# Gated DeltaNet in a hybrid recurrent step: the state chain gets a lane of its own, the block inverse moves into the preparation lane

## Chip, cores and metric

One NeuronCore of a Trainium2 chip runs the whole program. The metric is device time in microseconds (us), the median of several runs; lower is better. A profile of one execution, the trace, is read beside it.

## What is computed

One inference step of a two-layer trunk: 2048 prompt positions and 8 single-token samples, 1024 channels, float32. Layer 0 holds an RG-LRU and a gated DeltaNet as parallel groups of 8 heads behind one input projection and ahead of one output projection; layer 1 is an S5 state space layer. The change touches the DeltaNet of the prompt alone. For each head, with a decay `gc` (a running sum of log gates) and a factor `beta`:

```python
decay = exp(where(tri, gc[:, None] - gc[None, :], -inf))
A = where(strict, (k * beta) @ k.T * decay, 0)
u, w = solve(A + I, [v * beta, k * beta * exp(gc)])      # unit lower triangular
qk = where(tri, q @ k.T * decay, 0)
# chunk by chunk, S is the 128 x 128 state
v_new = u - w @ S
o = (q * exp(gc)) @ S + qk @ v_new
S = S * exp(g_last) + (k * exp(g_last - gc)).T @ v_new
```

## The kernel before

**Halves and heads.** The prompt is taken in two halves of 1024 positions. In layer 0 a half runs over 8 heads. Each head takes six units of the input projection in the order `k, xa, q, v, za, zb`, with the two gates of the RG-LRU (`lru`) between `za` and `zb`. A unit (`in_unit`) is 8 x 3 products of 128 x 128 weights with 1024 columns (1032 in the first half, with the 8 samples), since every float32 product is made of three products of high and low parts (`whi`, `wlo`; `hh`, `hl`). They are the matmuls at L840 into the PSUM tiles `ps_mm`. After the heads, `out_phase` runs 2 x 8 units of the output projection.

**Lanes.** Everything else is background: Python generators in the class `Fibers`, each in a lane. After every `BURST` = 1536 columns of a unit, `pump` advances the first generator of every lane by one `yield`; this is called a step here, and `wait(n)` is n steps. So a head of 6 x 24 x 1024 columns holds 96 steps. `drain` advances lanes to their end with no unit between the steps. Each engine takes its instructions in one fixed order, which a list scheduler makes of this program order.

**DeltaNet of a head** is in two generators. `gdn_prep` (lane `gp`) waits for `k`, transposes it (`ktok`), makes the decays `D`, the products `AT` (k with k) and `QKT` (k with q), each times `D`, then inverts the 16 x 16 diagonal blocks by forward substitution on VectorE (15 steps; `fsT`, `fsU`), writes them to scratch in HBM (`fst`), and reads them back in another layout by 16 small DMAs (`zt`, `zo`, `U32`), all on SyncE's queue. `gdn_main` (lane `gdn`) merges the inverse from blocks of 16 to 32, 64 and 128 by small matmuls into a tile `U`, and then goes over the 8 chunks, which depend on each other through the state `Sst`. At the end of each head stands `bg.drain("gp", "gdn")`; then `gdn_main` of this head is added, so that it runs during the next head.

**A chunk** is three hand-overs from TensorE to VectorE or ScalarE and back: p1 (L1094, L1095: k and q times the state), then `rr` on VectorE (L1097) and `qs` on ScalarE (L1100); two steps later p2 (L1103: the inverse times `rr`), then `wk` on VectorE (L1105) and `ww` on ScalarE (L1106); two steps later p3 (L1109, L1110), then the new state (L1111) and the output (L1112) on VectorE; three steps later the next chunk.

**Decays.** `decay_args` makes the exponents of the next head's `D` on VectorE (L874) behind the unit `za`, and the exponential is ScalarE's (L1157), in the middle of `lru`'s gate functions. The causal mask is put on `QKT` on GpSimd (`affine_select`, L949), behind VectorE's product at L948.

Of the kernel before, what the change touches and what calls it, by code (L numbers as in the profile page):

```python
# [26 lines left out]
DEC = 1  # L27
EVG = 3
# [5 lines left out]
class Fibers:  # L34
    """Background work, advanced step by step between bursts of the tensor engine."""
# [24 lines left out]
    def until(self, lane, flag, done):  # L60
        while flag not in done:
            self.step((lane,), True)
# [7 lines left out]
def hybrid_step(ctx: ExitStack, tc: tile.TileContext, I, O, dump=None):  # L70
# [46 lines left out]
    def in_order(*engines):  # L117
        """Each of these engines takes what the block traces in the order of the trace."""
# [19 lines left out]
    # ---------------------------------------------------------------- constants  # L138
# [25 lines left out]
    # ------------------------------------------------------------ small helpers  # L164
# [60 lines left out]
    # ------------------------------------------------------------- weight stream  # L225
# [50 lines left out]
    # --------------------------------------------------------------- parameters  # L276
# [115 lines left out]
    def make_h(i, xsrc, rows, hh, hl, permute, w):  # L392
        """h = rmsnorm(x) * w * (1 + scale) + shift, as two float32r parts."""
# [11 lines left out]
    def sample_norm(xs, name):  # L405
        """rstd of the sample rows, on every partition: [128, 8]"""
# [23 lines left out]
    # ---------------------------------------------------------------- S5 tables  # L430
    # Matrices of the 16-channel groups over 8 positions, kept in scratch by blocks of 8 groups.
# [22 lines left out]
    def s5_global():  # L454
# [35 lines left out]
        # powers 0..8 of the step  # L490
# [11 lines left out]
        # unit phases u^(2^j): j = 3 is the step of a chunk of 8  # L502
# [14 lines left out]
        # (A_bar - 1) / A  # L517
# [21 lines left out]
        # powers arranged by the rows' signs, in blocks of 8 groups  # L539
# [51 lines left out]
    def s5_tables(mt):  # L591
# [29 lines left out]
        for q in range(2):  # L621
# [28 lines left out]
            # phases of the chunks; the sine carries the rows' signs  # L650
# [30 lines left out]
    # ================================================================= layer 0  # L681
# [9 lines left out]
    tok = {n: K(n, (128, 8, 8)) for n in ("beta", "gc", "eg", "neg_eg", "egl", "ekap")}  # L691
# [19 lines left out]
    class Squares:  # L711
        """Sums of squares along the channels, by token columns."""
# [49 lines left out]
    def token_scalars(hf, Hh, Hl, blocks, wba):  # L762
# [41 lines left out]
        V.tensor_scalar(tok["neg_eg"], tok["eg"], -1.0, None, op0=OP.mult)  # L804
# [8 lines left out]
    def conv(dst, raw, wt, tile_i, silu, done=None):  # L813
        """the taps behind the last one"""
# [14 lines left out]
    def in_unit(hh, hl, blocks, evac, wts=None):  # L829
        """One block of 128 output channels; evac(first column, last column, sums)."""  # L830
# [18 lines left out]
    def raw_unit(unit, t, si, dst, wt, ti, bias=0.0):  # L849
        """channels before their convolution, and its last tap"""  # L850
# [14 lines left out]
    # ------------------------------------------------------------ gated DeltaNet  # L865
# [6 lines left out]
    def decay_args(dc, h):  # L872
        for c in range(8):
            V.tensor_scalar(dc[:, c], dc[:, c], tok["gc"][:, c, h:h + 1], 0.0, op0=OP.subtract, op1=OP.min)  # L874

    def gdn_prep(hf, h, g, ready):
        """Scalars, decayed products and inverses of the diagonal blocks of 16."""
# [29 lines left out]
        kap = g["kap"] = TT("gkap", S8)  # L907
# [1125 lines left out]
```

## Time and profile before

| | us |
|---|---|
| median of 3 runs | 3252.73 |
| lowest, highest | 3241.02, 3255.94 |
| span of the profiled execution, first to last instruction | 3234.9 |

The profile gives no time of its execution beside the span; the median is 17.8 us above it. Engines: PE is TensorE, PEld its weight loads, DVE VectorE, ACT ScalarE, POOL GpSimd, SP SyncE. In a view, "out<-in" names what an instruction writes and reads; an idle time in front of an instruction is put down to whoever released it last. "PEclk" is the clock granted to TensorE, as a share of 2.4 GHz.

### The profile page before, as it was taken

The numbers are of one execution on the slowest core, as the hardware profiler recorded it, in microseconds if no ns is written. First come the engines' busy times: TensorE is split into PE (matmuls) and PEld (weight loads), VectorE is DVE, ScalarE is ACT, GpSimd is POOL, SyncE is SP. The second block draws the span as 40 slices with busy tenths as digits, with TensorE's granted clock in tenths as the row PEclk, the third lists the DMA queues.
The fourth block names the chain that finished last, engine by engine and source line by source line (L and its number), as shares of the span: only waits on it lengthen the run. The fifth ranks groups of instructions, "written<-read, shape, count | busy, mean of one in ns | idle before, by whom it ended". The sixth has DMA issues, their size and how long they took to land. (4 is left out here: it accounts for less than half of the span.)

```text
span 3234.9 us, 53493 instructions
## 1 busy us (share of the span) xinstructions
PE 2980.9 (92%) x19958; PEld 2605.6 (81%) x19958; DVE 2207.5 (68%) x5420; ACT 1226.7 (38%) x2199; POOL 986.1 (30%) x872
## 2 busy tenths in 40 slices
PE   5898989999999999899999998999899999899998
PEld 3898988888888776677777777898888898778786
DVE  7887887578866777966776687445566734676634
ACT  3545544444443344534434444423111233211332
POOL 3224333333433424323323233322122223123231
PEclk8899999999999998999999999999999999999999
DMA  5132322322255532323322212433464414486322
GB/s 190 48 88 87 107 56 86 107 81 69 87 180 178 171 100 86 98 71 122 123 65 93 97 56 79 161 125 127 126 196 150 140 66 157 155 274 199 105 85 82
DMA packets 287780, 377.87 MB, mean 117 GB/s; under 512 B 97312, under 2 KB 165920, under 8 KB 287520
## 3 DMA queue, kind: packets, MB, share of 16 engines
q1 hardware_dynamic: 287520, 374.45, 35.6%
q8 instruction: 158, 2.59, 0.3%
q14 instruction: 102, 0.84, 0.1%
HBM read 276.73 MB, written 97.60 MB: 116 GB/s over the span
## 5 line engine op out<-in xcount | busy, mean ns | idle before, releaser
L218 POOL TENSOR_TENSOR wlo<-wraw,whi 128x512 fp32r<-128x512 f32 (+1 forms) x400 | 570.2, 1434 | 1207.3 <-ACT whi L217 729.9
L840 PE MATMUL ps_mm<-hh,wlo 128*128 128x512 f32 (+2 forms) x2536 | 793.2, 375 | 0.0
L840 PE MATMUL ps_mm<-hh,whi 128*128 128x512 f32 (+2 forms) x2536 | 758.6, 362 | 6.1 <-DVE acc L1197 2.9
L840 PE MATMUL ps_mm<-hl,whi 128*128 128x512 f32 (+2 forms) x2536 | 745.4, 356 | 0.8 <-DVE hl L402 0.8
L840 PEld LDWEIGHTS ps_mm<-hl,whi 128*128 128x128 f32 x2536 | 479.5, 192 | 47.4 <-DVE hl L402 1.4
L840 PEld LDWEIGHTS ps_mm<-hh,whi 128*128 128x128 f32 x2536 | 472.4, 192 | 55.8 <-DVE acc L1197 3.1
L840 PEld LDWEIGHTS ps_mm<-hh,wlo 128*128 128x128 f32 x2536 | 449.9, 193 | 35.2 <-issue 7.2
L217 ACT ACTIVATE whi<-wraw 128x512 fp32r<-128x512 f32 (+1 forms) x400 | 241.6, 618 | 181.3 <-DMA wraw<-in_w 50.6
L840 PE MATMUL ps_mm<-yh,whi 128*128 128x512 f32 (+2 forms) x640 | 186.0, 358 | 13.2 <-DVE acc L1197 6.9
L840 PE MATMUL ps_mm<-yl,whi 128*128 128x512 f32 (+2 forms) x640 | 187.3, 356 | 4.0 <-DVE stab L653 2.4
L840 PE MATMUL ps_mm<-yh,wlo 128*128 128x512 f32 (+2 forms) x640 | 190.9, 361 | 0.0
L1100 ACT ACTIVATE qs<-ps_ch,geg 128x128 f32<-128x128 f32 x128 | 46.9, 367 | 284.6 <-DVE rr L1097 281.5
L820 DVE SCALAR_TENSOR_TENSOR c_k<-raw,cbw,c_k 128x256 f32<-128x256 f32 x192 | 110.4, 614 | 61.5 <-ACT c_k L857 60.6
L840 PEld LDWEIGHTS ps_mm<-yh,whi 128*128 128x128 f32 x640 | 119.7, 192 | 26.3 <-DVE acc L1197 8.2
L840 PEld LDWEIGHTS ps_mm<-yl,whi 128*128 128x128 f32 x640 | 120.9, 192 | 15.8 <-DVE stab L653 2.8
L840 PEld LDWEIGHTS ps_mm<-yh,wlo 128*128 128x128 f32 x640 | 118.5, 192 | 9.1
L840 PE MATMUL ps_mm<-y2h,whi 128*128 128x384 f32 (+3 forms) x344 | 101.2, 341 | 9.4 <-DVE x L1866 9.4
L856 ACT ACTIVATE raw<-ps_mm 128x384 f32<-128x384 f32 (+1 forms) x160 | 81.5, 512 | 65.1 <-PE ps_mm L840 62.4
L820 DVE SCALAR_TENSOR_TENSOR xc<-raw,caw,xc 128x256 f32<-128x256 f32 x192 | 100.6, 544 | 4.5 <-ACT xc L857 3.9
L820 DVE SCALAR_TENSOR_TENSOR c_q<-raw,cbw,c_q 128x256 f32<-128x256 f32 x192 | 96.6, 537 | 5.2 <-ACT c_q L857 5.0
L840 PE MATMUL ps_mm<-y2l,whi 128*128 128x384 f32 (+3 forms) x344 | 99.6, 339 | 0.0
L840 PE MATMUL ps_mm<-y2h,wlo 128*128 128x384 f32 (+3 forms) x344 | 99.4, 338 | 0.0
(669 smaller groups left out, 5921.0 us busy)
## 6 DMA issues: line engine op xcount, KB each, us to landing
wraw<-in_w SPq DMA_DIRECT2D x256, 256.0 KB, 3.8
modw<-in_modw SPq DMA_DIRECT2D x48, 512.0 KB, 5.3
wraw<-in_wo SPq DMA_DIRECT2D x96, 256.0 KB, 3.7
yk<-yd SPq DMA_DIRECT2D x32, 512.0 KB, 5.6
xk<-x1d SPq DMA_DIRECT2D x32, 512.0 KB, 5.0
xk<-in_xt SPq DMA_DIRECT2D x24, 512.0 KB, 5.5
D<-gcd SPq DMA_DIRECT2D x16, 512.0 KB, 5.1
zd<-zbs SPq DMA_DIRECT2D x16, 512.0 KB, 3.9
```

The source lines that it names most:

```text
L217: a = A.activation(hi, src, AF.Identity)
L218: return a, (lo_eng or V).tensor_tensor(lo, src, f(hi), op=OP.subtract)
L820: V.scalar_tensor_tensor(d, raw[:, a * n + j:a * n + j + n], wt[:, tile_i, j:j + 1], d, op0=OP.mult, op1=OP.add)
L840: PE.matmul(p, w[:, c], x[:, b0:b1], start=(k == 0 and x is hh[k] and w is wh), stop=(k == 7 and w is wl))
L856: A.activation(raw[:, 3 + b0:3 + e], p[:, 0:e - b0], AF.Copy)
L1100: A.activation(qs, p1[:, 1, :], AF.Copy, scale=g["eg"][:, c:c + 1])
```

## The change

- `gdn_main` is split. The merges become `gdn_inverse`, called from `gdn_prep` (lane `gp`) between the work on `q` and that on `v`. They write into `AT` itself in place of a cleared tile `U`. The chunks and the output norm become `gdn_chain` (lane `gdn`), which begins when the preparation sets the flag `"U"`.
- The drain at the end of a head is gone. In its place, head h (from 2 on) steps both lanes, behind its unit `k`, until the chain of head h - 2 is done.
- The steps within a chunk are 3, 3, 4 in place of 2, 2, 3; for head 7 they stay 2, 2, 3.
- The forward substitution stands ahead of the work on `q`, six steps behind the products with k.
- `ktok` is scaled by `kap` beforehand, 8 ScalarE instructions for each head; so p3 takes `ww` alone, and `wk` on VectorE is gone. Signs are turned over so that `neg_eg` is not needed; two small copies go from VectorE to ScalarE.
- The mask is set in the exponents: one `affine_select` of 128 x 1024 on `D` between VectorE's exponents and ScalarE's exponential, in place of two of 128 x 512 on `QKT`.
- Comments are taken out, so lines have other numbers.

```diff
+CHAIN = ((3, 3, 4), (2, 2, 3))
...
     def decay_args(dc, h):
         for c in range(8):
             V.tensor_scalar(dc[:, c], dc[:, c], tok["gc"][:, c, h:h + 1], 0.0, op0=OP.subtract, op1=OP.min)
+        G.affine_select(dc, dc, pattern=[[0, 8], [1, 128]], compare_op=OP.is_ge,
+                        fill=-1000.0, base=0, channel_multiplier=-1)
...
+        for c in range(8):
+            A.activation(ktok[:, c], ktok[:, c], AF.Copy, scale=kap[:, c:c + 1])
+            if c % 4 == 3:
+                yield
+        yield from wait(6)
+         while "q" not in ready:
             yield
...
-            G.affine_select(QKT[:, qd * 4:qd * 4 + 4], QKT[:, qd * 4:qd * 4 + 4],
-                            pattern=[[0, 4], [1, 128]], compare_op=OP.is_ge,
-                            fill=0.0, base=0, channel_multiplier=-1)
             yield from wait(2)
...
-        for i in range(1, 16):
-            pr_ = TT("fsP", (64, 15, 15))
...
+        yield from gdn_inverse(AT, zt, zo, U32)
         while "v" not in ready:
             yield
...
+        ready.add("U")
+        yield
+    def gdn_inverse(U, zt, zo, U32):
-    def gdn_main(hf, h, g):
-        U = TA("U", FT, C3)
-        G.memset(U, 0.0)
...
+    def gdn_chain(hf, h, g, ready, waits):
+        while "U" not in ready:
+            yield
...
-            V.scalar_tensor_tensor(rr, p1[:, 0, :], g["neg_eg"][:, c:c + 1], vs[:, c, :],
-                                   op0=OP.mult, op1=OP.add)
+            V.scalar_tensor_tensor(rr, p1[:, 0, :], g["eg"][:, c:c + 1], vs[:, c, :],
+                                   op0=OP.mult, op1=OP.subtract)
...
-            yield from wait(2)
+            yield from wait(waits[0])
...
-            w, wk = TT("ww", (128, 128)), TT("wk", (128, 128))
-            V.tensor_scalar(wk, p2_, g["kap"][:, c:c + 1], None, op0=OP.mult)
+            w = TT("ww", (128, 128))
             A.activation(w, p2_, AF.Copy)
-            yield from wait(2)
+            yield from wait(waits[1])
...
-            PE.matmul(p3[:, 0, :], ktok[:, c, :], wk, start=True, stop=True)
+            PE.matmul(p3[:, 0, :], ktok[:, c, :], w, start=True, stop=True)
...
-            yield from wait(3)
+            yield from wait(waits[2])
...
-        yield from wait(10)
+        yield from wait(6)
...
                     bg.add(gdn_prep(hf, h, g, ready), "gp")
+                    bg.add(gdn_chain(hf, h, g, ready, CHAIN[h == 7]), "gdn")
+                    if h > 1:
+                        bg.until(("gp", "gdn"), ("gdn", hf, h - 2), done)
...
-            bg.drain("gp", "gdn")
-            bg.add(gdn_main(hf, h, g), "gdn")
```

**Where instructions stand, first place: TensorE within a chunk, first half.** `Sst` and `ps_ch` mark the chain; the rows between are the unit, two columns of blocks (384 each) in a row with x2. Before, from p2 (L1103) to p3 (L1109, L1110), with four transposes of `q` in between:

```order
L1103 MATMUL ps_ch<-rr,U 128x128
L958 MATMUL ps_pre<-ident,c_q 128x128 x4
L840 MATMUL ps_mm<-hh,wlo 128x384 x2
L840 MATMUL ps_mm<-hh,whi 128x384 x2
L840 MATMUL ps_mm<-hl,whi 128x384 x2
L1109 MATMUL ps_ch<-wk,ktok 128x128
L1110 MATMUL ps_ch<-ww,QKT 128x128
```

Of the change, p2 and p3 of a chunk, which are now L1115 and L1120, L1121:

```order
L1115 MATMUL ps_ch<-rr,AT 128x128
L840 MATMUL ps_mm<-hh,wlo 128x384 x2
L840 MATMUL ps_mm<-hh,whi 128x384 x2
L840 MATMUL ps_mm<-hl,whi 128x384 x2
L840 MATMUL ps_mm<-hh,wlo 128x384 x2
L840 MATMUL ps_mm<-hh,whi 128x384 x2
L840 MATMUL ps_mm<-hl,whi 128x384 x2
L1120 MATMUL ps_ch<-ww,ktok 128x128
L1121 MATMUL ps_ch<-ww,QKT 128x128
```

Between p2 and p3 stood 2304 columns of a unit here and stand 4608 now, and `wk` is no longer read. Over all 128 chunks the median number of unit columns in steps of 1536 goes from 2.0 to 3.0 between p1 and p2, from 2.0 to 2.9 between p2 and p3, and from 3.0 to 4.0 between p3 and the next p1.

**Second place: ScalarE around the gates of the RG-LRU, first half, head 4.** `ga`, `gx` and `tt` are the RG-LRU's, `D` the next head's decays, `zbs` the next unit's output. Before:

```order
L1153 ACTIVATE gx<-ps_mm,gxb 128x264
L1154 ACTIVATE tt<-ga,sp_538 128x1032
L1157 ACT_TABLE_LOAD
L1157 ACTIVATE D<-D 128x1024
L1155 ACTIVATE ga<-ga,spm_539 128x1032
L1158 ACT_TABLE_LOAD
L1158 ACTIVATE tt<-tt 128x1032
L634 ACTIVATE rt<-ps_pre 128x512
L1602 ACT_TABLE_LOAD
L1602 ACTIVATE zbs<-ps_mm 128x384 x2
```

Of the change, at the same place:

```order
L1165 ACTIVATE gx<-ps_mm,gxb 128x264
L1166 ACTIVATE tt<-ga,sp_537 128x1032
L1169 ACT_TABLE_LOAD
L1169 ACTIVATE D<-D 128x1024
L1167 ACTIVATE ga<-ga,spm_538 128x1032
L1170 ACT_TABLE_LOAD
L1170 ACTIVATE tt<-tt 128x1032
L1036 ACTIVATE U_5485<-ps_pre 16x8x16 x2
L1117 ACTIVATE ww<-ps_ch 128x128
```

A chunk's `ww` and a merge's copy now stand directly behind this block, while the p2 that `ww` reads stands among the gates' matmuls; p3, which takes `ww`, stands 13 steps of a unit behind that p2. In 13 of the 16 heads one chunk stands so (over 11 steps between p2 and p3, and `tt`'s square root between them on ScalarE); before, no chunk did.

**Third place: TensorE at the first merges, first half.** `ps_pre<-ident,c_q` is the last work on `q`, `ps_pre<-zt,AT` the first merge, in two groups of 16 that need different rows of `zt`. Of the change:

```order
L1120 MATMUL ps_ch<-ww,ktok 128x128
L1121 MATMUL ps_ch<-ww,QKT 128x128
L987 MATMUL ps_pre<-ident,c_q 128x128 x4
...
L1022 MATMUL ps_pre<-zt,AT 16x16 x16
L840 MATMUL ps_mm<-hh,wlo 128x264
L840 MATMUL ps_mm<-hh,whi 128x264
L840 MATMUL ps_mm<-hl,whi 128x264
L840 MATMUL ps_mm<-hh,wlo 128x264
L840 MATMUL ps_mm<-hh,whi 128x264
L840 MATMUL ps_mm<-hl,whi 128x264
L1022 MATMUL ps_pre<-zt,AT 16x16 x16
```

Before, the work on `v`, the end of the head and its drain stood between those two kinds of rows; now the merges follow the work on `q`, eight steps of the lane behind the end of the forward substitution.

## Rows read from the trace of the kernel before

**Rows 1.** The page: span, and busy time of two engines (share, count).

```profile
span 3234.9 us, 53493 instructions
PE 2980.9 (92%) x19958; PEld 2605.6 (81%) x19958; DVE 2207.5 (68%) x5420; ACT 1226.7 (38%) x2199; POOL 986.1 (30%) x872
```

**Rows 2.** Busy time by stage: heads, output phase, heads of the second half.

```profile
core 0: us, PE busy (x) PEld busy (x) DVE busy (x) ACT busy (x) POOL busy (x), PEclk, DMA share, GB/s
100.00:932.00 832.00, 771.00 (x6349) 723.11 (x6348) 677.05 (x1976) 399.56 (x788) 296.18 (x282) 0.98 0.27 84
932.00:1235.00 303.00, 289.05 (x1500) 232.23 (x1501) 220.88 (x529) 110.34 (x167) 115.53 (x106) 0.96 0.48 162
1235.00:2000.00 765.00, 713.36 (x4975) 560.06 (x4973) 552.08 (x1498) 334.25 (x615) 245.72 (x223) 0.97 0.29 91
```

**Rows 3.** Whom TensorE waited for: total us, times, longest us.

```profile
PE ps_ch L1103 <- DVE rr L1097: 36.5, 30, 3.3
...
PE ps_ch L1094 <- DVE Sst L1111: 10.8, 6, 3.1
...
PE ps_ch L1109 <- DVE wk L1105: 10.4, 13, 1.6
...
PE ps_pre L1017 <- DMA zt<-fst: 9.4, 3, 6.9
...
PE ps_pre L1017 <- DVE modr L365: 5.3, 1, 5.3
...
PE ps_pre L1046 <- DVE T L1035: 4.8, 4, 2.7
```

**Rows 4.** TensorE's matmuls by form, 300 to 400 us.

```profile
L840 PE MATMUL ps_mm<-hh,wlo 128*128 128x384 f32 x90 | 25.0, 357 | 0.0
...
L840 PE MATMUL ps_mm<-hh,wlo 128*128 128x264 f32 x48 | 14.3, 298 | 0.0
```

**Rows 5.** TensorE in order of time in a chunk (start, length; idle before).

```profile
318.57 0.39 PE L1095 MATMUL ps_ch<-Sst,c_q 128*128 128x128 f32 x2
...
319.15 0.51 PE L840 MATMUL ps_mm<-hh,whi 128*128 128x384 f32 x2
319.49 0.51 PE L840 MATMUL ps_mm<-hl,whi 128*128 128x384 f32 x2
...
321.05 0.49 PE L1103 MATMUL ps_ch<-rr,U 128*128 128x128 f32 x2 [0.70 <-DVE rr L1097]
```

**Rows 6.** Two instructions of the chain: ns shortest, median, longest.

```profile
L1105 DVE TENSOR_SCALAR wk<-ps_ch,gkap x128: 328/343/354, 199.2 to 2128.8; 128x128 f32<-128x128 f32 x128
L1106 ACT ACTIVATE ww<-ps_ch x128: 257/277/312, 199.6 to 2129.2; 128x128 f32<-128x128 f32 x128
```

**Rows 7.** SyncE's queue behind a forward substitution; then DMA issues, us to landing.

```profile
1704.13 0.55 SPq L114 DMA_DIRECT2D fst<-fsU  x1
...
1711.28 0.43 SPq L114 DMA_DIRECT2D zt<-fst  x1
fst<-fsU SPq DMA_DIRECT2D x16, 64.0 KB, 2.0
zt<-fst SPq DMA_DIRECT2D x64, 8.0 KB, 2.4
```

**Rows 8.** ScalarE at the gates in order of time, and L1157's waits in all.

```profile
477.40 0.59 ACT L1153 ACTIVATE gx<-ps_mm,gxb 128x384 f32<-128x384 f32 x1
...
484.47 1.06 ACT L1157 ACTIVATE D<-D 128x1024 f32<-128x1024 f32 x1 [2.36 <-DVE D L874]
...
487.88 1.06 ACT L1158 ACTIVATE tt<-tt 128x1032 f32<-128x1032 f32 x1
  DVE D L874: 34.2, 13
```

**Rows 9.** GpSimd by form, 100 to 2180 us.

```profile
L949 POOL TENSOR_SCALAR_AFFINE_SELECT QKT<-QKT 128x512 f32<-128x512 f32 x32 | 29.1, 916 | 144.7 <-DVE QKT L948 105.7 <-ACT raw L856 20.4 <-DVE halo L862 17.0
...
L1005 POOL MEMSET U<- 128x1024 f32 x16 | 15.4, 960 | 0.1
```

More of the change, by code (lines that the diff above doesn't have):

```diff
@@ L58, in pump, with until @@
             self.step()
-    def until(self, lane, flag, done):
+    def until(self, lanes, flag, done):
         while flag not in done:
-            self.step((lane,), True)
+            self.step(lanes, True)
     def drain(self, *lanes):
@@ L690, in hybrid_step @@
     Ps = K("Ps", (128, 48, 8))
-    tok = {n: K(n, (128, 8, 8)) for n in ("beta", "gc", "eg", "neg_eg", "egl", "ekap")}
+    tok = {n: K(n, (128, 8, 8)) for n in ("beta", "gc", "eg", "egl", "ekap")}
     x1d = D("x1d", (2, 8, 128, 1024))
@@ L906, in gdn_prep @@
         V.tensor_tensor(sj, sj, bt[:, :, h], op=OP.mult)
-        kap = g["kap"] = TT("gkap", S8)
+        kap = TT("gkap", S8)
         V.tensor_tensor(kap, sj, tok["ekap"][:, :, h], op=OP.mult)
-        for n in ("eg", "neg_eg", "egl"):
+        for n in ("eg", "egl"):
             g[n] = TT("g" + n, S8)
-            V.tensor_copy(g[n], tok[n][:, :, h])
+            A.activation(g[n], tok[n][:, :, h], AF.Copy)
         yield
@@ L939, in gdn_prep @@
         G.memset(Ti.rearrange("p a b -> p (a b)")[:, ::17], 1.0)
+        for c in range(8):
[3 more added lines that the diff above has]
+        yield from wait(6)
+        for i in range(1, 16):
+            pr_ = TT("fsP", (64, 15, 15))
+            s = (64, i, i)
+            V.tensor_tensor(pr_[:, 0:i, 0:i], Ti[:, 0:i, 0:i].rearrange("p j c -> p c j"),
+                            bc(F[:, 0:i, i].unsqueeze(1), s), op=OP.mult)
+            V.tensor_reduce(Ti[:, i, 0:i], pr_[:, 0:i, 0:i], axis=AX.X, op=OP.add, negate=True)
+            yield
+        Tu = TT("fsU", (64, 16, 16))
+        V.tensor_copy(Tu, Ti.rearrange("p i j -> p j i"))
+        dma(ft[0], Ti.rearrange("p i j -> p (i j)"))
+        dma(ft[1], Tu.rearrange("p i j -> p (i j)"))
+        zt, zo = TT("zt", (128, 8, 16)), TT("zo", (128, 8, 16))
+        U32 = TT("U32", (128, 8, 32))
+        G.memset(U32, 0.0)
+        fb = [ft[n].rearrange("(u b) (i j) -> b i u j", b=8, i=16) for n in range(2)]
+        for b in range(4):
+            r = 32 * b
+            dma(zt[r:r + 16], fb[0][2 * b])
+            dma(zo[r:r + 16], fb[1][2 * b + 1])
+            dma(U32[r:r + 16, :, 0:16], fb[1][2 * b])
+            dma(U32[r + 16:r + 32, :, 16:32], fb[1][2 * b + 1])
         while "q" not in ready:
@@ L1087, in gdn_main @@
         yield
+    def gdn_chain(hf, h, g, ready, waits):
+        while "U" not in ready:
+            yield
+        U, vs, ktok, QKT = (g[n] for n in ("AT", "vs", "ktok", "QKT"))
+        k, q = g["k"], g["q"]
         o = vs
@@ L1134, in gdn_main @@
             yield from wait(2)
+        done.add(("gdn", hf, h))
     def lru_split(xc, n):
@@ L1178, in load_y @@
             if grp == 1 and k == 7:
-                bg.drain("gdn")
+                bg.drain("gp", "gdn")
             y = TA("yk", FT, (128, n))
@@ L1620, in hybrid_step @@
         out_phase(hf, 0, oblocks, *ya, acc, (lb, *AH0))
-        bg.until("pro", ("sums", "mod")[hf], done)
+        bg.until(("pro",), ("sums", "mod")[hf], done)
         if hf == 0:
```

28 lines of the change are left out of this document (3 added, 25 removed).

## The prediction

> **What bounds the kernel now.** I read the page first: TensorE is busy for 2980.9 of 3234.9 us, and no other engine for more than 68% [rows 1]. The change takes no matmul away and adds none, so it can only move the time in which TensorE waits, or its clock. Next I read the stages, since the change touches layer 0 alone: in the two stretches of heads TensorE is idle for 832 - 771.0 = 61.0 and 765 - 713.4 = 51.6 us, in the first output phase for 14.0 [rows 2]. So 113 us of idle time is what can be won among the heads. The granted clock there is 0.98 and 0.97 of 2.4 GHz. As the levels are 1.2 and 2.4 GHz, that means 4% of 832 and 6% of 765 us at the low level, and at most half of these 33 + 46 us, 40 us, is lost to it.
>
> The chain of the profile ends in layer 1 and says little here, so I turned to TensorE's waits by releaser. The three hand-overs of a chunk cost 36.5 (30 waits for `rr`), 10.8 (6 for the state) and 10.4 (13 for `wk`), 57.7 us together; the first merge waits 9.4 us for `zt` and 5.3 for VectorE [rows 3]. That is two thirds of the 113 us. One chunk shows how it comes about: p1 ends at 318.96, four pairs of 384-column products run, and p2 starts 0.70 us late, behind `rr` [rows 5]. VectorE is busy for 677 of 832 us [rows 2], so `rr` queues there for longer than the two steps of cover.
>
> The Trainium skill (Perfetto Trace Analysis, section Identifying the Most-Contended Engine) says that matmul busy time is a poor measure of the headroom, and to take the weight loads' busy share. By the weight loads the heads hold 832 - 723 + 765 - 560 = 314 us [rows 2] of headroom, not 113, and a gain of the same share (26 of 113, below) would be 72 us. I stay with the waits, since rows of 384 to 512 columns cover a weight load without needing it to be busy; no run here has settled it.
>
> **How long a step is.** From 300 to 400 us, 90 rows of 384 columns and 48 of 264 stand for one of the three products [rows 4]; the other two have about as many. 3 x (90 x 384 + 48 x 264) = 141,700 columns are 92 steps of 1536, so a step is 1.09 us with its background work. Bare it is 4 rows of 384, and two take 0.34 us from start to start [rows 5]: about 0.70 us.
>
> **The change part by part.**
>
> *One step more in each hand-over.* If 30 waits of mean 1.2 us are spread evenly from 0 to 2.4, then 1.09 us more of cover takes 1.09 - 1.09²/4.8 = 0.84 from each, 25 us. The 6 waits for the state, from 0 to 3.6, lose 0.92 each, 5.5 us. Head 7 of each half keeps its steps, so 14/16 of this holds: 26.7. The waits for `wk` go with `wk`, 10.4: `ww` takes 0.277 us and came behind `wk`'s 0.343 [rows 6]. Sum 37. Bounds: with bare steps of 0.70 it is (18 + 3.7) x 14/16 + 10 = 29; all of it is 57.7. I take **-37**.
>
> *VectorE and GpSimd.* VectorE loses 128 x 0.343 = 44 us [rows 6], 2.7 us a head; GpSimd loses 15.4 us of clearing `U`, and its masks change from 32 x 0.916 to 16 of twice the size, between 15 and 29 us [rows 9]. ScalarE gains 128 scalings, at `ww`'s 0.277 [rows 6] 35 us; at 400 of 832 us busy [rows 2] it has room. None is TensorE's work: 0, except where it makes something late, below.
>
> *No drain, merges elsewhere.* The waits of the first merges at the head's end, 9.4 + 5.3 [rows 3], lose their place; of the next merge's 4.8 us for VectorE's transpose [rows 3] I take the drain's share at 3: **-18** (bounds -9, the DMA's alone, and -19.5, all three).
>
> *What the merges wait for now.* They follow the end of the forward substitution by 8 steps of the lane, their second group by 9: 8.7 and 9.8 us. VectorE lags behind TensorE by about 2 us, estimated from the waits for `rr` [rows 3], so the second group comes 7.8 us after the substitution. It needs the fourth `zt`. In a quiet queue that one is issued 7.15 us behind the write of `fsU` and lands 2.4 later, 9.6 [rows 7]. So TensorE waits for some 1.5 us; in the 12 heads in which the order has about this distance, **+18**. Bounds: 0, and 12 x 5 = 60 when weights or decays stand among the 16 reads in SyncE's queue.
>
> The Trainium skill (DMA: Bandwidth & Descriptors, section Anatomy of one DMA) gives a fixed cost of about 2.0 us for a transfer, dominated by its completion. For the single transfer the trace agrees (2.0 and 2.4 us to landing [rows 7]); a write and a read would then be back after 4 us, ahead of the merges, and this term would be 0, the sum 18 us lower. The row decides otherwise, since 16 reads are issued one after another.
>
> *`ww` behind the gates.* In 13 heads a chunk's `ww` now stands behind ScalarE's gate functions. From the end of the `gx` at 477.40, by which p2 stands, to the end of the square root at 488.94 is 10.95 us, of which 2.36 is a wait for VectorE's exponents [rows 8]; two merge copies and `ww` make about 11.7. p3 stands 13 steps behind p2, 9.1 us bare, and with the merges' small matmuls about 10.8. So TensorE waits 0.9 us, 13 times: **+12**. The mask adds 0.92 to 1.83 us of GpSimd between exponents and exponential [rows 9], VectorE's 2.7 us less of work takes as much away. Bounds: 0, and 13 x 2.7 = 35.
>
> *Start of the output phase.* Chain 7 of each half now runs where the unit waits for its inputs `yh`; its covers there are short. 16 chunks at 0.3 us, a wait of rows 5 halved, are **+5** (0 to 12).
>
> *Clock.* Fewer long waits; of 40 us at most, **-6** (0 to -20), since the new waits are as long as some of the old.
>
> Slots: both programs fill all 35 of the large tiles' slots at times; I set 0, up to +15.
>
> **Sum.** -37 - 18 + 18 + 12 + 5 - 6 = -26 us on the span of 3234.9, 3208.9. The median lies 17.8 above that span; with the same on top the forecast is **3226.7 us**, 0.8% faster. Differences under 0.5%, 16 us, are about what a measurement of this kernel can't tell from none.
>
> **Rivals.**
>
> *A, slower: the reads come back late.* For: SyncE also issues weights, decays and table traffic, and a read behind them is late for all merges; TensorE takes its instructions in order. Against: by [rows 7] the quiet queue is only 1.5 us late. With 5.3 us in each of 12 heads the term is 64 in place of 18: -26 + 46 = +20, 3273 us. It decides from 5.0 us a head on.
>
> *B, no change: ScalarE's block.* If the mask's 1.83 us come on top and VectorE is no earlier, p3 waits 2.7 us, 35 in place of 12, and the rest of the sum is -3: 3250 us. For: ScalarE waited 34.2 us for the exponents already, 13 times [rows 8]. Against: they are VectorE's, which has less to do.
>
> *C, more gain: the new waits are hidden.* If reads are back in time and ScalarE's block ends before p3, 18 + 12 go, and the clock gives back 20 rather than 6: -70, 3183 us. For: a wait anywhere on TensorE lets VectorE and ScalarE catch up, so waits don't add. Against: the orders put the merges close behind their reads. By the rule on weight loads of the Trainium skill (Perfetto Trace Analysis, section Identifying the Most-Contended Engine) it would be 72.
>
> *D, it doesn't do what it says:* p2 could stay two steps behind p1, if the scheduler put it there. The order shows three, so I give it nothing.
>
> **How the numbers follow.** The forecast's own case, 17 to 50 us faster, gets 0.42; C 0.20; B, within 16 us, 0.20; A 0.18. So faster 0.62, same 0.20, slower 0.18. The forecast's own range is 3203 to 3236. The range for 8 in 10 reaches into C (-80, 3172) and A (+14, 3266).
>
> **What would show it.** Right: TensorE's waits for `rr` under 15 us in all, for the state under 6, none for `wk`; idle time among the heads near 85 us. Waits of the merges for `zt` near 18 us and of p3 for `ww` near 12 confirm the new terms; if both are near 0 it is C, if `zt` is over 60, A, if `ww` is over 30, B. It would be wrong if TensorE's busy time changed by more than its clock, or if long waits stood where heads meet, behind `until`: the chain takes 8 x 10 + 11 of a head's 96 steps, so little is left.

## The result: slower by 1%

| | before | changed |
|---|---|---|
| median, us | 3254.34 (4 runs) | 3281.52 (4 runs) |
| lowest to highest, us | 3241.02 to 3258.89 | 3278.47 to 3282.24 |
| span of the profiled execution, us | 3234.9 | 3276.7 |
| mean granted clock, share of 2.4 GHz | 0.967 | 0.959 |

The ratio of the times is 1.0096, 95% interval 1.0073 to 1.0120: 27 us lost where I forecast 26 won. The profiled executions differ by 41.8 us, since the one of before lay under its own runs.

The page of the changed kernel, span and busy times:

```profile
span 3276.7 us, 53366 instructions
PE 3021.6 (92%) x19958; PEld 2643.2 (81%) x19958; DVE 2095.6 (64%) x5242; ACT 1264.5 (39%) x2358; POOL 970.1 (30%) x840
```

Beside [rows 1]: TensorE is idle for 3276.7 - 3021.6 = 255.1 us; it was 254.0. The same 19958 matmuls are busy for 40.7 us longer. So no waiting was won or lost on balance; TensorE ran more slowly. The two granted clocks say by how much. Span times clock, roughly the time that it would take if all of it ran at the high level, is 3234.9 x 0.967 = 3128.1 before and 3276.7 x 0.959 = 3142.4 now. Of the 41.8 us, 14.3 are left; 27.5 are the clock.

This pair overstates the clock's part in the loss between the medians. In 80 further executions of the kernel before, taken beside the experiments, the mean granted clock lay between 0.954 and 0.972 with a median of 0.963, and span times clock had a median of 3127; the four executions of the changed kernel have 0.958 or 0.959, and 3142 to 3146. So some 15 of the 27 us between the medians are not the clock, and some 12 are.

Busy time by stage, at borders that stand at the same matmuls of the units as in [rows 2], and the stretch behind them:

```profile
100.20:959.80 859.60, 798.09 (x6482) 750.89 (x6481) 626.65 (x1899) 421.47 (x879) 293.85 (x274) 0.95 0.27 82
959.80:1262.50 302.70, 287.95 (x1378) 230.74 (x1378) 213.20 (x525) 107.94 (x163) 102.26 (x92) 0.96 0.49 160
1262.50:2033.80 771.30, 724.00 (x4974) 571.20 (x4972) 501.28 (x1413) 353.41 (x688) 245.23 (x213) 0.96 0.29 90
2033.80:2219.60 185.80, 174.48 (x1189) 159.40 (x1188) 88.06 (x194) 66.15 (x113) 47.53 (x50) 0.97 0.37 125
```

In the heads TensorE is idle for 859.6 - 798.1 = 61.5 and 771.3 - 724.0 = 47.3 us, 108.8 where it was 112.6 [rows 2]; I had forecast 85. The clock fell from 0.98 to 0.95 and from 0.97 to 0.96: by the trace's clock records, 137.5 us at 1.2 GHz in place of 70.0. That is where the time went in this pair: the two stretches are 27.6 and 6.3 us longer, the output phase between them is not (302.7 and 303.0), and half of TensorE's busy time at the low level, my estimate of what that level costs, rose by 33.2 us in the two (from 31.2 to 64.4). The other 8 us lie behind them, in the second output phase and in layer 1, which the change doesn't touch. VectorE has 101 us less to do in the two stretches, and TensorE waits for it as long as before.

TensorE's waits in the changed kernel (whom for: total us, times, longest):

```profile
PE ps_ch L1105 <- DVE Sst L1122: 29.1, 22, 3.4
PE ps_ch L1115 <- DVE rr L1109: 28.7, 35, 2.2
...
PE ps_pre L1139 <- DVE c_v L1134: 17.8, 9, 4.7
...
PE ps_pre L987 <- DVE QKT L980: 13.1, 5, 6.1
...
PE ps_ch L1120 <- ACT ww L1117: 4.6, 4, 2.4
...
PE ps_pre L1022 <- DMA zt<-fst: 1.7, 3, 1.3
```

In [rows 3], `rr`, the state and `wk` held up TensorE for 57.7 us together. `wk` is gone, and the other two are at 57.8. The merges' waits for `zt` fell from 9.4 to 1.7. The waits of the transposes of the output `o` behind its norm (L1139) rose from 2.2 to 17.8 us, and those of the transposes of `q` behind QKT's product (L987) from 1.7 to 13.1.

One place shows a wait and what it sets off: TensorE by windows (columns as in [rows 2]), then TensorE and VectorE in order of time:

```profile
461.00:468.90 7.90, 5.89 (x39) 5.58 (x39) 6.61 (x22) 4.01 (x10) 4.34 (x3) 1.00 0.14 48
468.90:475.70 6.80, 6.20 (x24) 6.20 (x25) 6.76 (x20) 0.37 (x1) 1.66 (x3) 0.50 0.21 78
```

```profile
466.39 0.51 PE L840 MATMUL ps_mm<-hh,wlo 128*128 128x384 f32 x2
469.50 0.80 PE L1105 MATMUL ps_ch<-Sst,c_k 128*128 128x128 f32 x2 [2.60 <-DVE Sst L1122]
...
472.08 0.99 PE L840 MATMUL ps_mm<-hh,whi 128*128 128x384 f32 x2
```

```profile
465.24 0.47 DVE L820 SCALAR_TENSOR_TENSOR c_v<-raw,cbw,c_v 128x256 f32<-128x256 f32 x1
465.63 0.26 DVE L955 TENSOR_REDUCE fsT<-fsP 64x11 f32<-64x121 f32 x1
465.82 1.32 DVE L820 SCALAR_TENSOR_TENSOR c_v<-raw,cbw,c_v 128x256 f32<-128x256 f32 x1
468.20 0.17 DVE L859 COPY Ps<-ps_mm 128x8 f32<-128x8 f32 x1 [1.05 <-ACT c_v L857]
...
469.11 0.33 DVE L1122 SCALAR_TENSOR_TENSOR Sst<-Sst,gegl,ps_ch 128x128 f32<-128x128 f32 x1
```

The state of this chunk is behind convolution taps of `v` and rows of the forward substitution in VectorE's order, and VectorE itself waits 1.05 us for ScalarE. TensorE stands for 2.60 us, and for the next 6.8 us the clock is at the low level: pairs of 384 columns take 0.84 to 0.99 us where they took 0.51.

### The profile page after: what moved, and what is told of

It is laid out like the page before. It is cut to its first block, busy times and chain, and to the rows that moved or that the text cites. A ratio compares the mean times of both kernels' runs of the same rounds, so it can differ in the third digit from the quotient of the medians.

```text
span 3276.7 us, 53366 instructions
## 1 busy us (share of the span) xinstructions
PE 3021.6 (92%) x19958; PEld 2643.2 (81%) x19958; DVE 2095.6 (64%) x5242; ACT 1264.5 (39%) x2358; POOL 970.1 (30%) x840
## 5 line engine op out<-in xcount | busy, mean ns | idle before, releaser
L840 PE MATMUL ps_mm<-hh,whi 128*128 128x512 f32 (+2 forms) x2536 | 766.8, 364 | 10.8 <-ACT c_v L857 4.3
L840 PE MATMUL ps_mm<-hl,whi 128*128 128x512 f32 (+2 forms) x2536 | 757.7, 360 | 0.8 <-DVE hl L403 0.8
L840 PEld LDWEIGHTS ps_mm<-hh,wlo 128*128 128x128 f32 x2536 | 458.5, 194 | 34.2 <-issue 5.6
L820 DVE SCALAR_TENSOR_TENSOR c_k<-raw,cbw,c_k 128x256 f32<-128x256 f32 x192 | 99.8, 558 | 13.7 <-ACT c_k L857 12.9
```

Of the source, the lines that this page charges most:

```text
L820: V.scalar_tensor_tensor(d, raw[:, a * n + j:a * n + j + n], wt[:, tile_i, j:j + 1], d, op0=OP.mult, op1=OP.add)
L840: PE.matmul(p, w[:, c], x[:, b0:b1], start=(k == 0 and x is hh[k] and w is wh), stop=(k == 7 and w is wl))
```

## The experiments

All labels in one table, by the median and the ratio to the kernel before on the same chip (its medians there: 3242 to 3248 us); clock and idle time of TensorE (span minus busy) are from the profiled execution.

| run | us | ratio, 95% interval | clock | idle |
|---|---|---|---|---|
| e1_wait9 | 3289.57 | 1.0127, 1.0098 to 1.0155 | 0.957 | 264.8 |
| e2_gaps_short | 3271.54 | 1.0075, 1.0052 to 1.0097 | 0.959 | 248.4 |
| e3_old_order | 3257.93 | 1.0024, 1.0008 to 1.0040 | 0.963 | 249.6 |
| e4_drain_back | 3350.00 | 1.0324, 1.0294 to 1.0353 | 0.945 | 273.8 |
| b1_arith | 3231.97 | 0.9959, 0.9939 to 0.9978 | 0.961 | 244.6 |
| b2_cover | 3395.27 | 1.0456, 1.0417 to 1.0494 | 0.931 | 291.6 |
| e5_structure | 3277.80 | 1.0093, 1.0064 to 1.0121 | 0.964 | 268.3 |
| e7_spread | 3294.84 | 1.0138, 1.0098 to 1.0179 | 0.961 | 254.5 |
| e8_merges_last | 3320.22 | 1.0241, 1.0203 to 1.0278 | 0.942 | 253.6 |
| e9_subst_late | 3398.23 | 1.0480, 1.0449 to 1.0511 | 0.930 | 278.8 |
| b3_inplace | 3262.71 | 1.0055, 1.0034 to 1.0075 | 0.956 | 255.2 |
| e10_head6 | 3283.70 | 1.0120, 1.0084 to 1.0156 | 0.957 | 261.3 |
| e12_after_u | 3308.74 | 1.0186, 1.0151 to 1.0221 | 0.955 | 267.9 |
| e13_order_u | 3263.50 | 1.0041, 1.0022 to 1.0059 | 0.962 | 252.0 |
| b4_kap | 3248.74 | 0.9995, 0.9976 to 1.0014 | 0.965 | 253.2 |
| b5_mask | 3239.32 | 0.9971, 0.9951 to 0.9991 | 0.962 | 246.1 |
| f1_after_nostate | 3300.54 | 1.0176, 1.0146 to 1.0206 | 0.956 | 263.7 |
| f2_before_nostate | 3244.41 | 1.0008, 0.9990 to 1.0026 | 0.965 | 253.0 |

### Is it the new waits of the output's transposes?

```diff
-        yield from wait(6)
+        yield from wait(9)
         for b in range(NB):
```

> The changed kernel with 9 steps in place of 6 between the output norm and the transposes of o (before had 10). Theory W (the waits of these transposes for the norm, 17.8 + 4.1 us in the changed kernel, and the low clock behind them are the loss): these waits fall under 8 us and the median falls by 15 to 25 us, to about 3262. Theory G (the longer gaps spread the chain over the stretches in which VectorE is crowded): the waits for the state and rr stay at 58 us together and the median moves by less than 8 us. Theory D (the merges now run beside the chain's end, and many small matmuls at once lower the clock): no change either, the granted clock stays at 0.96.

This run also has 9 steps in place of 10 at one place each of `token_scalars` and of layer 1's `s5`, outside the lane in question, so its time is not that of the one edit alone. The waits at L1139 for the norm fell only from 17.8 to 13.8 us, other waits rose, and the time is 0.3% above the changed kernel's ratio, within what the intervals allow as no change. Theory W fell: these waits shrank by 4 us and nothing was gained.

### Are longer gaps worth anything?

```diff
-CHAIN = ((3, 3, 4), (2, 2, 3))
+CHAIN = ((2, 2, 3), (2, 2, 3))
```

> The changed kernel with gaps of 2, 2 and 3 steps in every head. Theory G: the chain ends 24 steps earlier, so the waits for rr and the state do not rise (58 us together, or less) and the median is 15 us or more below the changed kernel's 3281. Cover theory (of the prediction: a step more of cover is worth 27 us): the waits for rr and the state rise by 20 us or more, to 80, and the median is 3300 or more. Theory W: the transposes of o no longer meet the merges, their waits fall under 8 us, and the median falls by 15 us whatever the chain's waits do.

TensorE's waits in this run:

```profile
PE ps_ch L1115 <- DVE rr L1109: 34.4, 36, 4.4
PE ps_ch L1105 <- DVE Sst L1122: 21.7, 15, 4.0
PE ps_pre L1139 <- DVE c_v L1134: 18.5, 12, 2.8
```

34.4 + 21.7 = 56.1 us with a step less in each gap, 57.8 with it. The cover theory wanted 80 and 3300 us; the median is 3271.5. So three longer gaps together took nothing off these waits. The gain of 10 us over the changed kernel is less than theory G wanted, and the two intervals overlap.

The same question in the kernel before, a step more between p1 and p2 alone:

```diff
-            yield from wait(2)
+            yield from wait(3)
             p2_ = PS("ch", (128, 128))
```

> The kernel before with one edit: three steps in place of two between p1 and p2 (gaps 3, 2, 3). Cover theory of the prediction (0.84 us from each of 30 waits for rr, 25 us): the waits for rr fall from 36.5 to 12 us and the median falls by 15 to 25 us. Queue theory (rr stands later in VectorE's fixed order when it is given more steps, so the wait doesn't shrink): the waits for rr stay at 30 us or more and the median stays within 8 us of before.

By the ratio, 148 us slower, which neither theory had. TensorE's waits in this run:

```profile
PE ps_pre L1128 <- DVE c_v L1123: 48.6, 12, 7.6
PE ps_ch L1109 <- DVE wk L1105: 31.3, 29, 2.5
PE ps_ch L1094 <- DVE Sst L1111: 19.2, 14, 4.1
...
PE ps_ch L1103 <- DVE rr L1097: 8.4, 7, 3.4
```

The step of cover did to `rr` what the cover theory said: its waits fell from 36.5 to 8.4 us, where I had expected 12. But those for the state rose from 10.8 to 19.2 and those for `wk` from 10.4 to 31.3. The three are 58.9 us together, where they were 57.7 [rows 3]: the wait moved to the next hand-overs (in a run that the drain slows as well).

The time itself went elsewhere, into the waits at L1128, the transposes of `o` behind the norm. The lane of the kernel before had only two or three steps of a head to spare. Counting the steps in the program's generators:

```
steps of the drain behind heads 0 to 7, first half
kernel before     0  0  0  0  0  0  0  0
b2_cover          0  5  5  6  5  5  5  6
e4_drain_back    17 10 10 11 11 10 10 11
```

Eight steps more in a head leave 5 or 6 to the drain, the transposes of `o` among them, where no unit runs beside them, and the clock of the whole run is 0.931. The first row matters more: **the drain that the change removes was empty**, in all 16 heads, and `until` in its place takes no step either. Put back into the changed kernel, with the chain behind it, it would not be empty:

```diff
-                    bg.add(gdn_chain(hf, h, g, ready, CHAIN[h == 7]), "gdn")
-                    if h > 1:
-                        bg.until(("gp", "gdn"), ("gdn", hf, h - 2), done)
...
             dma(zd[h % 2], zb)
+            bg.drain("gp", "gdn")
+            bg.add(gdn_chain(hf, h, g, ready, CHAIN[h == 7]), "gdn")
```

> The changed kernel with the drain between heads put back and the chain of a head begun behind it, so that it runs beside the next head's k, xa, q; gaps 3, 3, 4, merges still in the preparation's lane. If the absence of the drain costs (the chain's end beside the next merges, theory D), the granted clock rises to 0.965 or more and the median falls by 15 us or more. If the drain was a loss, as the prediction had it (18 us), the waits of the first instructions in a drain come back and the median rises by 10 to 20 us, to 3295.

3350 us: the rest of the preparation, the last merges and the transposes of `v`, is now drained. The first reading had the wrong sign, and the second was too small. It shows that the changed lanes need the missing drain, not that the drain of before cost anything.

### Which edits gain, which lose

The arithmetic alone, in the kernel before (its core; the two copies, the missing `neg_eg` and the mask as in the change's diff):

```diff
+            A.activation(ktok[:, c], ktok[:, c], AF.Copy, scale=kap[:, c:c + 1])
...
-            V.tensor_scalar(wk, p2_, g["kap"][:, c:c + 1], None, op0=OP.mult)
...
+        G.affine_select(dc, dc, pattern=[[0, 8], [1, 128]], compare_op=OP.is_ge,
+                        fill=-1000.0, base=0, channel_multiplier=-1)
```

> The kernel before with the arithmetic edits alone: ktok scaled by kap beforehand, no wk, signs turned over, the two small copies on ScalarE, the mask in the exponents. Lanes, drain, order and gaps as before. The prediction's step (the waits for wk, 10.4 us, go with it, and VectorE has 44 us less to do): median 5 to 15 us below before. Rival (VectorE's freed time isn't on the path, and ww or the mask's place in front of the exponential cost as much): within 5 us of before. If the arithmetic is what made the change slow: 10 us or more above before.

> The kernel before with ktok scaled by kap beforehand and no wk, nothing else. The prediction's 10.4 us of waits for wk: the median falls by 5 to 12 us. If the waits only pass to ww: within 4 us of before.

> The kernel before with the mask in the exponents and none on QKT, nothing else. The prediction gave it nothing but a share in the wait for ww: within 4 us of before. If the two selects between QKT's product and the chain were on the path, 5 us or more below; if the select ahead of the exponential holds up ScalarE, 5 us or more above.

Together they are 0.4% faster than before: this part alone beats both kernels. `kap` by itself gives nothing (0.9995), though the waits for `wk` are gone: those for the state are now 15.5 us and those of p3 for `ww` 7.5, with `rr`'s 35.7 together 58.7, where the three of before had 57.7. The mask by itself gives 0.3%, as the second reading of its run had it.

Next the new lanes with short gaps and the old order of the preparation (e3, its diff against e2, of which only lines at their new places are shown), and the same with `wk`, the selects on QKT and a cleared tile `U` put back (e5):

```diff
         while "q" not in ready:
             yield
...
+        for i in range(1, 16):
+            pr_ = TT("fsP", (64, 15, 15))
...
         while "v" not in ready:
             yield
...
+        yield from gdn_inverse(AT, zt, zo, U32)
         ready.add("U")
```

> As the run with gaps of 2, 2 and 3 in every head, and the order in the preparation as before: forward substitution behind the work on q, merges behind the work on v (still in the preparation's lane and in place). If the order in the preparation costs something (waits of the transposes of q for QKT's product, 13.1 + 2.8 us in the changed kernel), these waits fall under 4 us and the median is 8 us or more below that of the run with short gaps alone. If it does not, the two agree within 8 us.

> The run with short gaps and the old order of the preparation, with the arithmetic put back as before (wk, mask on QKT behind the product, ktok not scaled, U a tile of its own and cleared): what is left of the change is no drain and the merges in the preparation's lane. If the arithmetic is worth 10 us, this is 10 us above that run, at 3268; if the arithmetic is worth nothing, the two agree within 6 us, and so lane and drain cost some 10 us against before.

With short gaps and the old order the kernel comes back to 1.0024, and the waits for QKT's product to 2.1 us, so the new order costs 0.5% (e2 against e3). The same without the arithmetic and with a tile `U` stands at 1.0093. Its partner with the arithmetic is e13 (below; a tile `U` too), at 1.0041, so the arithmetic is worth 0.4% (b1) to 0.5%. The new lanes lose 0.8% on top of the arithmetic (e13 against b1) and 0.9% without it (e5 against before), both with a tile `U`; with the inverse in place they lose nothing (e3 against b3, below: 1.0024 and 1.0055, intervals that overlap). e5 loses its 0.9% at a granted clock of 0.964, about that of before, so the clock is not what the lanes cost there.

Read as one path from the kernel before to the changed one, the ratios are 0.9959 with the arithmetic (b1), 1.0041 with the new lanes (e13), 1.0024 with the inverse in place (e3), 1.0075 with the new order (e2) and 1.0096 with the longer gaps: -0.4, +0.8, -0.2, +0.5 and +0.2%. The third and the last step lie within the intervals. On this path the lanes and the order are what loses; on another the shares differ, as the inverse in place shows.

Taking back one half of the order at a time is far worse than either whole (e8: merges behind `v` only; e9: substitution behind `q` only, merges ahead of `v`):

> The run with gaps of 2, 2 and 3 in every head, with one thing of the old order back: the merges behind the work on v (the forward substitution stays ahead of q). If it is the merges' place beside the gate products and the chain's end that lowers the clock (51 us more at the low clock in the heads of the first half than before), the low stretches in the heads go back to those of before within 15 us and the median falls from 3271 to about 3258, that of the run with the old order. If it is the place of the forward substitution, the median stays within 5 us of 3271.

> The other half: gaps of 2, 2 and 3, the forward substitution behind the work on q as before, the merges six steps behind it and ahead of v as in the changed kernel. If the merges' place decides, the median stays at 3265 or more and the low clock of the heads stays; if the substitution's place decides, 3258 or less. The merges wait more for zt here (six steps are 6.5 us, less than the 9.6 us that the reads take): 20 us or more of such waits, in either theory.

Both theories of these runs fell. The trace of e9 shows one place, TensorE in order of time and by windows:

```profile
402.17 1.94 PE L1140 MATMUL ps_pre<-ident,c_v 128*128 128x128 f32 x8 [5.39 <-DVE c_v L1135]
```

```profile
399.00:405.00 6.00, 2.83 (x11) 2.42 (x11) 4.39 (x10) 0.00 (x0) 0.87 (x1) 0.55 0.41 138
405.00:409.80 4.80, 4.80 (x103) 3.67 (x102) 0.00 (x0) 2.05 (x7) 0.57 (x2) 0.85 0.75 233
409.80:437.10 27.30, 27.30 (x197) 23.39 (x197) 7.11 (x20) 9.53 (x23) 7.47 (x9) 0.50 0.17 55
437.10:442.00 4.90, 4.90 (x31) 4.87 (x31) 2.27 (x5) 0.37 (x1) 0.16 (x1) 1.00 0.02 3
```

A wait of 5.39 us for the norm, then the merges, 16 x 16 and 32 x 32 products among the unit's: 27.3 us without an idle moment at the low clock. It comes back when the merges are over. In e9 twelve low stretches last 13.7 to 30.7 us, 256 us together. In the changed kernel the same happens with no wait ahead of it:

```profile
488.00:498.00 10.00, 10.00 (x89) 9.72 (x88) 1.83 (x9) 9.73 (x13) 3.51 (x2) 1.00 0.16 55
498.00:503.00 5.00, 5.00 (x63) 4.60 (x61) 3.23 (x7) 2.95 (x8) 3.87 (x5) 1.00 0.14 52
503.00:513.00 10.00, 10.00 (x92) 8.68 (x92) 7.57 (x19) 4.29 (x8) 4.75 (x3) 0.50 0.26 93
513.00:523.00 10.00, 10.00 (x81) 8.65 (x79) 3.84 (x11) 4.14 (x10) 3.62 (x3) 0.99 0.68 214
```

TensorE is busy for all of these 35 us. Behind 498 stand the second group of merges and, beside it, p3 of a chunk and transposes of the table lane; from 503 the clock is at 0.50 for 10 us.

How much is that? From 100 us to the end of the second half's heads, the kernel before has 15 stretches at the low level, 95.6 us in all, and in the 5 us ahead of each TensorE idles for more than 1.1 us. The changed kernel has 24 such, 126.3 us, and six more, 37.5 us, ahead of which it idles for 0.44 us at most. Half of the busy time in the six, some 19 us, is what they cost by estimate. Five of the six begin behind merges. But merges do not lower the clock by themselves. In the kernel before, one head's 128 products of 16 x 16 stand within 6.3 us, with TensorE busy throughout, and the clock stays at 1.00 there and behind (by windows):

```profile
275.00:281.30 6.30, 6.30 (x149) 5.46 (x148) 6.30 (x7) 2.91 (x9) 4.14 (x3) 1.00 0.51 200
281.30:290.00 8.70, 8.70 (x109) 8.05 (x105) 4.61 (x8) 3.85 (x10) 4.34 (x6) 1.00 0.40 127
```

What has to stand beside the merges is not shown.

Spreading the merges (short gaps, two steps in place of one at five places of the inverse):

```diff
-            yield
+            yield from wait(2)
```

> The run with gaps of 2, 2 and 3 in every head, and the merges twice as far apart: two steps in place of one at five places of the inverse. Theory D (the merges of 16 and 32 rows side by side with the other lanes' small matmuls lower the granted clock without any wait): the low stretches without a wait ahead of them go, the granted clock rises from 0.959 to 0.963 or more, and the median falls by 8 us or more below 3271. Theory W (only waits lower the clock): no change of the clock, within 5 us.

The clock rose a little (0.961), yet the time is 0.6% longer than that of the run with short gaps, so what it lost is not the clock; that a longer stretch of merges meets more of the rest is a guess. Theory D in this simple form fell.

### Does the inverse in place decide?

```diff
-        U = TA("U", FT, C3)
-        G.memset(U, 0.0)
+        U = AT
```

> The kernel before with the arithmetic edits, and the inverse in place as well (no tile U, no clearing of it on GpSimd, 16 x 0.96 us), lanes and order as before. If slots or GpSimd's clearing mattered: 5 us or more below the run with the arithmetic alone (3232). If not: within 4 us of it, and this is the part of the change that can be kept.

> The changed kernel with one edit undone: the inverse goes into a tile U of its own, cleared on GpSimd, as before. If the inverse in place costs here what it cost in the kernel before (31 us, from 3232 to 3263), the median falls to about 3250. If that cost belongs to the old lanes alone, the median stays within 8 us of 3281.

> The run with short gaps and the old order of the preparation (3258), with a tile U of its own: all that is left of the change is the arithmetic, the lanes and the missing drain. If the parts add up, 31 us less, 3227, which would be below the kernel before and below the arithmetic alone (3232). If not, 3250 or more.

In the kernel before (with the arithmetic) it costs 31 us; undone in the changed kernel it costs another 27 (1.0186 against 1.0096); undone in the short version with the old order, nothing (1.0041, 1.0024). None of the readings of the first two runs had this; of the third, the second reading came. Part of the first is seen at the start of the output phase. TensorE's merges with a tile `U` of its own (b1), in order of time:

```profile
931.44 1.19 PE L1058 MATMUL ps_pre<-U,X 32*32 32x32 f32 x32
...
952.73 0.63 PE L1068 MATMUL ps_pre<-ident,U 64*64 64x64 f32 x8
```

its clock behind the first of them by windows:

```profile
937.40:952.00 14.60, 14.60 (x64) 11.62 (x63) 6.82 (x6) 5.76 (x7) 0.00 (x0) 1.00 1.02 397
```

and in place (b3), with the clock of the whole stretch:

```profile
933.28 1.30 PE L1057 MATMUL ps_pre<-U,X 32*32 32x32 f32 x32
...
936.51 1.06 PE L1067 MATMUL ps_pre<-ident,AT 64*64 64x64 f32 x8
```

```profile
923.80:951.10 27.30, 24.54 (x198) 17.49 (x195) 9.36 (x13) 11.07 (x25) 11.15 (x14) 0.50 0.57 194
```

With `U` the scheduler put 21 us of unit products between the merges to 32 and those to 64, and the clock is back at 1.00 there, after 13.7 us at the low level; in place they follow after 3.2 us, and it stays at the low level for 27.3 us. Both stretches begin behind waits. The program has the same steps between the merges in both; the gap is the scheduler's. The clock is not all of it: by the mean clocks the low time rises from 252 to 287 us, at most 18 of the 35.7 us between the two profiled executions, and TensorE's idle time rises by 10.6.

The chain of head 6 was a suspect at the same place:

```diff
-                    bg.add(gdn_chain(hf, h, g, ready, CHAIN[h == 7]), "gdn")
+                    bg.add(gdn_chain(hf, h, g, ready, CHAIN[h >= 6]), "gdn")
```

> The changed kernel with the short gaps (2, 2, 3) for head 6 of each half too, so that its chain is done 24 steps earlier, before the output phase begins. If the chain of head 6 and its output norm in the first units of the output phase are what costs there (these stretches are 11.5 and 5.6 us longer than before in the trace), the two stretches fall by 10 us together and the median to about 3270. If it is head 7's own merges and chain: no change, within 4 us of 3281.

No change within the intervals (1.0120 against 1.0096): not the cause.

### Take the state's waits away

```diff
-            PE.matmul(p1[:, 0, :], k[:, t0:t0 + 128], S, start=True, stop=True)
-            PE.matmul(p1[:, 1, :], q[:, t0:t0 + 128], S, start=True, stop=True)
+            PE.matmul(p1[:, 0, :], k[:, t0:t0 + 128], ident, start=True, stop=True)
+            PE.matmul(p1[:, 1, :], q[:, t0:t0 + 128], ident, start=True, stop=True)
```

> The changed kernel with k and q multiplied by the identity in place of the state, so that the first products of a chunk wait for no earlier chunk. It leaves out the state's way into the output; all instructions are still there. Theory S (the waits for the state, 29.1 us in 22 waits where there were 10.8 in 6, and the low clock behind them are the loss): the median falls by 35 to 50 us, to about 3240, and comes within 10 us of the same edit in the kernel before. Theory O (the loss lies in the other lanes' work, merges and transposes): it falls by no more than 15 us more than the kernel before does with the same edit.

> The kernel before with the same edit (identity in place of the state; leaves out the state's way into the output). Its 10.8 us of waits for the state go: 10 to 20 us below before, in either theory.

The waits for the state are gone in both, and neither is faster: the kernel before is where it was (1.0008), against what I expected of it in either theory, and the changed kernel is 0.8% slower with the edit than without (1.0176 against 1.0096), which theory O's bound allows and does not explain. TensorE's waits, the changed kernel with this edit, then the kernel before with it:

```profile
PE ps_ch L1115 <- DVE rr L1109: 49.6, 39, 4.7
```

```profile
PE ps_ch L1103 <- DVE rr L1097: 46.3, 34, 4.5
```

Before: 36.5 + 10.8 = 47.3 us for `rr` and the state [rows 3], now 46.3 for `rr` alone. Changed: 57.8, now 49.6, and the wait for `ww` doubles from 4.6 to 9.2. What one hand-over no longer waits, the next one does, as in b2 and b4. Theory S fell, and with it every sum of waits taken one by one.

## Why the prediction was wrong

Two steps of the sum failed by the most: the 37 us for the longer hand-overs came to nothing, and the clock, which I had at 6 us won, cost some 33 us among the heads of the profiled pair (half of TensorE's busy time at the low level) and some 12 of the 27 us between the medians. Term by term:

- **One step more in each hand-over, -37: failed.** I took each wait as a lateness of fixed length that a step of cover shortens by 0.84 us. `rr` and the state wait for 57.8 us in place of 47.3, and e2 has about the same with a step less. b2 shows the step: one more step of cover took 28 us off the waits for `rr`, more than I had taken, and the next two hand-overs waited 29 us more. b4 and f2 show it again; b4 loses the waits for `wk` and gains nothing. The runs suggest that VectorE's place in time sets the sum; none changes that alone. My words under rival C, that a wait lets the others catch up, come nearest, and I had used them for one rival alone.
- **No drain, -18: failed in its premise.** The drain took no step, so its waits were those of ordinary merges. They did fall when these moved (9.4 to 1.7 for `zt`), and 30.9 us of waits stand at L1139 and L987 where 3.9 stood, for which I had no term. I should have counted the drain's steps first.
- **Merges wait for `zt`, +18: too large, 1.7.** By my own rows it should have read 9.6 - 7.8 = 1.8 us a head, 21 in all, and not 1.5. The reads were about as late as I had worked out: the write of `fsU` at 475.23 and the fourth `zt` at 482.06, 6.83 us behind; it was 7.15 in [rows 7].

```profile
475.23 0.46 SPq L115 DMA_DIRECT2D fst<-fsU  x1
...
482.06 0.43 SPq L115 DMA_DIRECT2D zt<-fst  x1
```

  TensorE came later than 9 steps of 1.09 us: here the last products of the second group begin at 486.50, 11.3 us behind the write. The sum by the Trainium skill (DMA: Bandwidth & Descriptors, section Anatomy of one DMA) had 0 here and is nearer, but for another reason: a read back after 4 us is not what the trace shows of the fourth read. That section describes transfers that GpSimd issues, and these are SyncE's; for one transfer the trace agrees with it all the same (1.9 us to landing for the write, 1.8 for a read, in the changed kernel).
- **`ww` behind the gates, +12:** right in kind, 4.6.
- **Start of the output phase, +5:** not told apart by a run; the first output phase as a whole is as long as before. The longest low stretch of the changed kernel lies there, around a wait of 4.71 us at L1139 (by windows):

```profile
953.60:970.70 17.10, 12.66 (x52) 9.26 (x53) 9.74 (x22) 3.12 (x6) 3.56 (x3) 0.50 0.57 190
```

- **Clock, -6: failed, +27.5 between the profiled executions.** I tied it to the length of the waits. But the idle time among the heads hardly changed, and yet 24 low stretches begin behind waits where 15 did; and the six without a wait, 37.5 us, I had not thought of. The change puts merges beside the chain, the gate products and the transposes of `o`; that this mixture is the cause of the six is likely from where they stand, and not shown.
- **Slots, 0:** not separated; e12 and e13, which use one tile more, are 27 and 6 us slower than their partners.

Of the signs that I had named, the one for `wk`, no waits, held. `rr` under 15, the state under 6 and 85 us of idle time did not; TensorE's busy time rose by 40.7 us, of which its clock explains 27.5 or more, so the first of my signs of being wrong came in part. `until` took no step, so no wait stood behind it. Rival A is the nearest in time, 3273, by a mechanism that did not occur.

Over all 20 profiled executions, before and changed among them, the spans run from 3230.8 to 3395.2 us, 164 apart, and TensorE's idle time from 244.6 to 291.6, 47 apart. Span times clock runs from 3104.8 (b1) to 3165.3 (e4), 60 apart. In the four slowest (b2, e4, e8, e9), with clocks of 0.930 to 0.945, most of the loss is the clock. In the other 16 it is a part: their spans are 73 apart, and span times clock is still 58 apart (3104.8 to 3162.3). b1 is faster than the kernel before, and its clock is no higher.

What stays open: the 14.3 us that the clock doesn't explain; what lowers the clock where TensorE doesn't wait; and why the parts don't add (in place: +31 and -27). Each edit gives another scheduler's order, and I have no run that holds the order fixed while one wait or one group of merges is changed.

## What to carry to other kernels

A wait for an engine that is behind may only move when it is asked later: in this kernel the waits of one hand-over passed to the next. So sum the waits for one engine and ask what makes that engine earlier, and count what a removed drain really does before giving it a price. Where idle time stays and busy time grows, read the granted clock stretch by stretch, see what stands there, and ask first how far the clock of one kernel scatters between its executions. Try the parts alone: here the mask and the pre-scaling in the old lanes are faster than either kernel.

## What the hardware showed that I had not expected

- The granted clock went to 0.50 with TensorE busy all the time (10 us from 503 in the changed kernel), when 16 x 16 and 32 x 32 products and 128 x 128 transposes stood among the unit's; and it stayed there through 27.3 us of such a mixture in e9 (TensorE busy throughout) and in b3 (24.5 of the 27.3). The same merges at 275 us of the kernel before left it at 1.00.
- A wait of 2.60 us was followed by 6.8 us at the low level (from 468.9), by estimate 3.1 us lost, half of the 6.20 in which TensorE was busy: as much behind the wait as in itself.
- An extra step of cover took 28.1 us off the waits for `rr` (36.5 to 8.4) and put 29.3 us onto the waits for the state and `wk`.
